# First norm with its mean in PSUM, later norms and a convolution reworked around PSUM

## The chip, the cores and the metric

The kernel runs on one core of a Trainium2 chip. The metric is device time in microseconds of one execution; the time before is 1544.75 us, the median of three runs (1543.83, 1544.75 and 1547.15). A core has five engines, each with an instruction queue of its own that runs in order: PE (TensorE, with its weight loads shown as PEld), DVE (VectorE), ACT (ScalarE), POOL (GpSimd) and SP, which issues most of the DMAs. Engines wait for each other through semaphores.

## The reference

One step of a decoder with two layers, for 512 prompt positions and 8 x 8 sample positions, 576 tokens in all, with a model width of 1024. Layer 0 mixes with RWKV-7 and retention heads, layer 1 with a gated convolution; each mixer is followed by a squared-ReLU MLP, and each of the four residual sums by a layer norm. Cut to what the change touches:

```python
def layer_norm(x, g, b):
    mu = jnp.mean(xf, -1, keepdims=True)
    var = jnp.mean(jnp.square(xf - mu), -1, keepdims=True)
    return ((xf - mu) * lax.rsqrt(var + LN_EPS)).astype(x.dtype) * g + b

def conv_mixer(x, buf0, w_in, conv_w, w_out):
    bg, cg, h = jnp.split(x @ w_in, 3, axis=-1)
    u = cg * h
    ext = jnp.concatenate([buf0.astype(u.dtype), u], axis=1)
    conv = sum(ext[:, j:j + T] * conv_w[j] for j in range(CONV_W))
    return (bg * conv) @ w_out, ext[:, ext.shape[1] - (CONV_W - 1):]

# trunk, for layers l = 0 and 1
x = layer_norm(ALPHA * x + y, ln1_g[l], ln1_b[l])            # norms 0 and 2
x = layer_norm(ALPHA * x + sqrelu_mlp(x, w_up[l], w_down[l]), ln2_g[l], ln2_b[l])   # norms 1 and 3
```

## The kernel before

**Layout.** Features lie on partitions: `T.x` is eight row tiles of 128 features x 576 tokens, and most work goes by halves of the tokens, g = 0 and 1, of 288 each (`GN`). An f32 product is made of three matmuls of a rounded high part and a low part (`mm3`): high x high, high x low, low x high. Each operand is therefore split, as a rule by a cast on ScalarE (L77) and a subtraction on VectorE (L78), and both parts are kept.

**Order of the work.** Layer 0's mixers run until about 430 us; their instructions are placed by hand-written generators. The scheduler of the framework then orders each engine's queue by priorities and its own estimate of times, so a change of a few instructions can reorder a queue beyond the lines that the diff names. The output projection (`Wout`) runs among the mixers in three parts, over the input blocks k = 0 to 2, 3 to 5, and 6, and adds into `T.x`; the last block, k = 7, is done at the start of the trunk with the weights `w7`, together with the first norm. Then come MLP 1, norm 1, the convolution's input projection (three columns of row tiles by an ordinary product, the other six in nine seven-product steps), its output projection with norm 2, MLP 2, and norm 3, whose outputs leave by DMA.

**The first norm.** Because a mean over features is linear in the weights, `means` takes the column means of the weights of k = 6 and 7, and these are subtracted from the weights (`less`), so what those blocks add has no mean. `center`, run after the second part, sums the eight row tiles with matmuls against a constant 1/1024 (L1395) and subtracts the result from `T.x` (L1396). In the trunk, `ln0_add` (L289) adds each product of k = 7, squares the sum on ScalarE (L291), adds pairs of squares on POOL (L294) and sums over features with an f32 matmul against 1/1024 (L283). `ln0_finish` makes the factor and scales.

**Norms 1 to 3.** `ln_add` takes the row tiles as they are finished (L257), and adds up both the tiles and their squares on POOL and VectorE (L273); one matmul against 1/1024 for each of the two sums turns these into mean and mean square in PSUM. `ln_finish` copies the mean out of PSUM (L322), makes the factor v, subtracts the mean (L341), multiplies by v on VectorE or POOL (L342) and applies gain and offset on ScalarE (L345), followed by the split.

**Seven products.** `gemm7` makes two row tiles for both token halves from seven products of half the depth (12 matmuls each) in place of eight. Every product has a PSUM bank of its own, out of six; two are copied to SBUF on ScalarE (L207, L213), and the sums are built in SBUF by five adds on VectorE and two on POOL (all L205). In the convolution an `evac` function is then called on the two finished tiles `ta` and `tb`: a gate (kept), the product u = gate x h with the convolution behind it on ScalarE and VectorE (L1721 to L1723), or the product with the third tile, which is split for the output projection.

Of the kernel before, what the change touches and what calls it, by code (L numbers as in the profile page):

```python
# [16 lines left out]
P = 128  # L17
# [7 lines left out]
class Trunk:  # L25
# [124 lines left out]
    def mm3(self, acc, hi, lo, xh, xl, first, last):  # L150
        nc = self.nc
        nc.tensor.matmul(acc, lhsT=hi, rhs=xh, start=first, stop=False)  # L152
        nc.tensor.matmul(acc, lhsT=hi, rhs=xl, start=False, stop=False)  # L153
        nc.tensor.matmul(acc, lhsT=lo, rhs=xh, start=False, stop=last)  # L154
# [68 lines left out]

    def ln_state(self, n, x):
        return {'n': n, 'x': x}
# [37 lines left out]
    def ln_sum(self, st, n, m, g, t, direct, onv):  # L263

        nc = self.nc
        if m in direct:
            self.ln_mm(st, n, g, t, m == KT - 1 and (g, n) not in st)
# [7 lines left out]
        if m == KT - 1 and (g, n) in st:  # L275
            self.ln_mm(st, n, g, st[g, n], True)
# [8 lines left out]
    def ln0_add(self, st, m, g, r, a):  # L285

        nc = self.nc
        st[g, m] = r
        nc.vector.tensor_tensor(out=r, in0=r, in1=a, op=ALU.add)  # L289
        t = self.p_tmp.tile([P, GN], F32, tag="t", name="lt", bufs=self.tb)  # L290
        nc.scalar.activation(t, r, AF.Square)  # L291
        if m >= 6: self.ln_mm(st, 'q', g, t, m == 7)
        elif m % 2:
            nc.gpsimd.tensor_tensor(out=t, in0=st[g, 'q'], in1=t, op=ALU.add)  # L294
            self.ln_mm(st, 'q', g, t, False)
        else: st[g, 'q'] = t
# [19 lines left out]

    def ln_finish(self, st, g, par, out, last=False):
        nc = self.nc
# [995 lines left out]
CFG = {(n, g): dict(ds=() if n else tuple(range(8)), dq=() if n else tuple(range(8)), sv=(7,), qv=(7,), pg=(1, 2, 3, 4, 5, 6, 7), mulv=(0, 3, 6), affv=()) for n in range(4) for g in range(2)}  # L1314
# [11 lines left out]
class Wout:  # L1326


    def __init__(self, T, w):
        self.T, self.nc, self.w = T, T.nc, w  # L1330
        self.w7, self.less = [], {}
# [12 lines left out]
    def weights(self, m, k0, n):  # L1344

        t = self.slot()
        b = self.less.get(k0)
        if b is None:
            t = t[:, 0:n]
            self.nc.sync.dma_start(t.rearrange('p m c -> p (m c)'), self.w[30 + m, :, P * k0:P * (k0 + n)])  # L1350
        else:
            n = 2
            self.nc.sync.dma_start(t, self.w[30 + m:32 + m, :, P * k0:P * (k0 + 1)].rearrange('m p c -> p m c'))
            self.nc.scalar.activation(t, t, AF.Identity, bias=b)
        hi, lo = (self.wq.tile([P, 2, P], F32R, tag=f'w{c}', name=c, bufs=3)[:, 0:n] for c in 'hl')
# [4 lines left out]
    def means(self):  # L1360
# [3 lines left out]

        def load(k, m):
            t = self.slot()
            nc.sync.dma_start(t, self.w[30 + m:32 + m, :, P * k:P * (k + 1)].rearrange('m p c -> p m c'))
            return t
        for k in (6, 7):
            s = self.wq.tile([P, 4], F32, name=f's{k}', bufs=1)  # L1370
            for m in range(0, 8, 2):
                t = load(k, m)
                nc.vector.tensor_reduce(out=s[:, m // 2:m // 2 + 1], in_=t, axis=AX.XY, op=ALU.add)
            b = self.wq.tile([P, 1], F32, name=f'b{k}', bufs=1)
            nc.vector.tensor_reduce(out=b, in_=s, axis=AX.X, op=ALU.add)
            nc.vector.tensor_scalar(out=b, in0=b, scalar1=-1.0 / 1024, scalar2=None, op0=ALU.mult)
            self.less[k] = b
        for m in range(0, 8, 2):
            t = load(7, m)
# [6 lines left out]
    def center(self, mx):  # L1386
# [3 lines left out]
        nc.gpsimd.memset(o, 1 / 1024)  # L1390
        for g in range(2):
            ps = mx.tile([P, 512], F32, tag='mx', name='mx')[:, 0:GN]
            xs = [t[:, GN * g:GN * (g + 1)] for t in T.x]
            for m, t in enumerate(xs):
                nc.tensor.matmul(ps, lhsT=o, rhs=t, start=m == 0, stop=m == KT - 1)  # L1395
# [405 lines left out]
```

## Time and profile before

| | |
|---|---|
| runs | 1543.83, 1544.75, 1547.15 us |
| profiled execution | 1545.83 us, of which the span takes 1544.1 |
| mean granted clock of TensorE | 0.972 |
| first norm, from the last block's stall to the MLP's first matmul | 472.8 to 512.09 us |
| norm 1, second half | 911 to 929 us |
| convolution's seven-product steps | about 970 to 1070 us |
| norm 3, last product to last DMA | 1526.5 to 1544.1 us |

A row of the profile gives the line of the kernel, the engine, the operation, the tiles it writes and reads, and their size; a bracket at its end gives the time that the engine stood idle before it and what it waited for. In a table of waits a row gives the total in microseconds, the number of waits and the longest. Matmuls are pipelined: one of 128x288 is shown with 0.29 us, but the next starts 0.13 us after it.

### The profile page before, as it was taken

What the parts mean: (1) busy time and instruction counts of PE and PEld (TensorE: products, weight loads), DVE (VectorE), ACT (ScalarE), POOL (GpSimd) and SP (SyncE); (2) the same over time, 40 slices, a digit from 0 to 9 for tenths busy, and PEclk for the clock granted to TensorE, in tenths of its full rate; (3) what the DMA queues carried; (4) which work ended last, traced back from release to release, by engine and by line L of the source; (5) the groups of instructions that cost most, each with busy time, mean ns of one, the idle gap of its engine ahead of it and who ended that gap; (6) DMA issues with size and microseconds to landing.
All of it is one profiled execution on the core that took longest, in us unless ns stands there. A gap on an engine that the chain in (4) does not pass through costs nothing.

```text
span 1544.1 us, 29826 instructions
## 1 busy us (share of the span) xinstructions
PE 1464.9 (95%) x11744; PEld 1414.5 (92%) x11744; DVE 1072.2 (69%) x2040; ACT 643.6 (42%) x1355; POOL 547.9 (35%) x619
## 2 busy tenths in 40 slices
PE   6999999999997899999999989999989999999995
PEld 6998898989786899999999989989989999999995
DVE  4655676766868884855748689899799475574845
ACT  4433334233343851523525454334366253351533
POOL 2032213346442531212113665554682131121355
PEclk9999999999998999999999999999999999999998
DMA  5332334445322131322313302223304223142211
GB/s 173 98 97 86 94 97 132 137 115 168 117 61 81 42 123 55 100 93 70 123 56 111 122 1 69 83 83 113 109 1 123 69 83 110 55 127 66 96 56 62
DMA packets 73244, 141.08 MB, mean 91 GB/s; under 512 B 21744, under 2 KB 33248, under 8 KB 73104
## 3 DMA queue, kind: packets, MB, share of 16 engines
q1 hardware_dynamic: 70272, 130.74, 27.4%
q0 software_dynamic: 1536, 5.57, 1.1%
q10 hardware_dynamic: 1296, 2.86, 0.5%
q8 instruction: 92, 1.51, 0.4%
q14 instruction: 48, 0.39, 0.1%
HBM read 125.44 MB, written 13.70 MB: 90 GB/s over the span
## 4 chain that ended last, share of the span: by engine, by line
PE 73%; DVE 11%; issue 5%; POOL 4%; DMA 4%; ACT 2%; SPq 1%; DVEq 0%; ACTq 0%; POOLq 0%
PE acc L152 20%; PE acc L153 20%; PE acc L154 20%; DVE wl L78 3%; PE mx L835 2%; DMA raw<-in_w 1%; POOL x L255 1%; DVE u L341 1%; PE mx L732 1%; POOL ts L1653 1%; PE mx L574 1%; PE wa L152 1%; ACT wh L77 1%; POOL ln L273 1%; PE mx L524 1%
## 5 line engine op out<-in xcount | busy, mean ns | idle before, releaser
L77 ACT CAST wh<-raw 128x512 fp32r<-128x512 f32 x440 | 252.7, 618 | 421.1 <-PE acc L153 271.0
L78 DVE TENSOR_TENSOR wl<-raw,wh 128x512 fp32r<-128x512 f32 x440 | 334.0, 791 | 42.0 <-ACT wh L77 35.0
L153 PE MATMUL acc<-hl,wh 128*128 128x288 f32 x1180 | 348.9, 297 | 0.0
L154 PE MATMUL acc<-hh,wl 128*128 128x288 f32 x1180 | 348.6, 296 | 0.0
L152 PE MATMUL acc<-hh,wh 128*128 128x288 f32 x1180 | 346.2, 297 | 1.9 <-DVE ta L205 1.8
L152 PEld LDWEIGHTS acc<-hh,wh 128*128 128x128 f32 x1180 | 221.0, 188 | 2.8 <-DVE ta L205 2.0
L153 PEld LDWEIGHTS acc<-hl,wh 128*128 128x128 f32 x1180 | 222.2, 188 | 0.5
L154 PEld LDWEIGHTS acc<-hh,wl 128*128 128x128 f32 x1180 | 222.2, 188 | 0.3
L152 PE MATMUL acc<-xh,wh 128*128 128x288 f32 x480 | 147.7, 309 | 14.1 <-ACT xh L1482 12.4
L153 PE MATMUL acc<-xl,wh 128*128 128x288 f32 x480 | 145.6, 304 | 0.0
L123 POOL TENSOR_TENSOR s<-raw 128x512 f32<-128x512 f32 x37 | 52.0, 1405 | 264.0 <-DMA raw<-in_w 197.6
L154 PE MATMUL acc<-xh,wl 128*128 128x288 f32 x480 | 145.5, 303 | 0.0
L153 PE MATMUL acc<-lt,wh 128*128 128x288 f32 x444 | 131.8, 297 | 3.6 <-DVE lt L78 3.6
L154 PE MATMUL acc<-ht,wl 128*128 128x288 f32 x444 | 131.6, 296 | 0.9 <-DVE wl L78 0.9
L152 PE MATMUL acc<-ht,wh 128*128 128x288 f32 x444 | 131.3, 296 | 0.1
L123 POOL TENSOR_TENSOR raw<-raw 128x512 f32<-128x512 f32 x37 | 54.9, 1484 | 158.9 <-DVE raw L123 106.4
L152 PEld LDWEIGHTS acc<-xh,wh 128*128 128x128 f32 x480 | 90.9, 190 | 17.7 <-ACT xh L1482 12.7
L152 PE MATMUL acc<-ho,wh 128*128 128x288 f32 x352 | 104.6, 297 | 0.1
L154 PE MATMUL acc<-ho,wl 128*128 128x288 f32 x352 | 104.6, 297 | 0.0
L153 PE MATMUL acc<-lo,wh 128*128 128x288 f32 x352 | 104.5, 297 | 0.0
L153 PEld LDWEIGHTS acc<-xl,wh 128*128 128x128 f32 x480 | 90.9, 189 | 2.5 <-DVE xl L1483 0.7
L154 PEld LDWEIGHTS acc<-xh,wl 128*128 128x128 f32 x480 | 91.0, 190 | 1.5 <-issue 0.2
(485 smaller groups left out, 3466.6 us busy)
## 6 DMA issues: line engine op xcount, KB each, us to landing
raw<-in_w SPq DMA_DIRECT2D x160, 512.0 KB, 3.6
raw<-in_w SPq DMA_DIRECT2D x60, 256.0 KB, 2.9
la<-in_w SPq DMA_DIRECT2D x32, 128.0 KB, 2.2
A<-stg SPq DMA_DIRECT2D x9, 288.0 KB, 2.5
x<-in_x POOLq DMA_DIRECT2D x8, 288.0 KB, 5.8
out_y<-x SPq DMA_DIRECT2D x16, 144.0 KB, 1.8
kr<-A SPq DMA_DIRECT2D x6, 288.0 KB, 2.8
lr<-in_x ACTq DMA_DIRECT2D x4, 288.0 KB
```

Of the source, the lines that this page charges most:

```text
L77: a = self.nc.scalar.copy(hi[:, s], src[:, s])
L78: b = self.nc.vector.tensor_tensor(out=lo[:, s], in0=src[:, s], in1=hi[:, s].bitcast(F32), op=ALU.subtract)
L123: tt = lambda e, o, x, y, op: e.tensor_tensor(out=o, in0=x, in1=y, op=op)
L152: nc.tensor.matmul(acc, lhsT=hi, rhs=xh, start=first, stop=False)
L153: nc.tensor.matmul(acc, lhsT=hi, rhs=xl, start=False, stop=False)
L154: nc.tensor.matmul(acc, lhsT=lo, rhs=xh, start=False, stop=last)
L255: e.tensor_tensor(out=t, in0=t, in1=c, op=ALU.subtract)
L273: (nc.vector if m in onv else nc.gpsimd).tensor_tensor(out=o, in0=st[g, n], in1=t, op=ALU.add)
L341: nc.vector.tensor_tensor(out=u, in0=r, in1=mn, op=ALU.subtract)
L524: self.nc.tensor.matmul(out, lhsT=src, rhs=self.C['ident'][q, q], start=True, stop=True)
L574: self.nc.tensor.matmul(ps, lhsT=lhsT, rhs=rhs[:, o:o + n], start=True, stop=True)
L835: nc.tensor.matmul(ps[:, i], lhsT=bd(self.mb if n < 3 else self.Y0, j + i), rhs=v[:, j + i], start=True, stop=True)
```

## The change

Six edits, all around where a sum is held.

1. `means` computes the column means of the weights of k = 7 only. The weights of k = 6 are no longer centred.
2. `center` runs after the third part of the output projection, so the mean is that of all of k = 0 to 6. It is not subtracted from `T.x`: it is split into a high and a low part (`W.mean`), and in the trunk each product of k = 7 begins with two matmuls of a negated identity (`W.neg`) by these parts, so the mean is subtracted in PSUM.
3. The squares of the first norm are all summed on TensorE, row tile by row tile; POOL's adds are gone.
4. In norms 1 to 3, for the second half of the tokens, the row tiles 6 and 7 and their squares go straight to TensorE; the sum of tiles 0 to 5 is added as before.
5. For that half `ln_finish` is replaced by `ln_end`: mean and factor stay in PSUM, the row tile is changed in place, and no product is left to POOL. The first half keeps the old way.
6. The convolution's nine steps use `chained7`: products that are added to each other are accumulated onto the same bank, three banks for seven products, with copies of what stands in between on ScalarE, three adds on VectorE and none on POOL. The last sum is read from PSUM by `evac`. The copies of the new convolution state go from POOL to ScalarE.

`mm3` is written more shortly and issues the same matmuls. The core of the diff:

```diff
@@ Trunk
+    def chained7(self, u, x7, evac):
...
+        a = product(0, bank())
+        nc.scalar.copy(s1, a)
+        c = product(3, bank())
+        nc.scalar.copy(s5, c)
+        product(2, a, False)
+        nc.scalar.copy(u2, a)
+        product(5, c, False)
+        add(ta[:, r], c, u2)
+        product(4, a, False)
+        add(tb[:, r], a, s5)
+        b = product(1, bank())
+        add(ta[:, l], b, s1)
+        evac(0, ta, None)
+        product(6, a, False)
+        evac(1, tb, a)
@@ ln_add
-        if m == KT - 1 and (g, n) in st:
-            self.ln_mm(st, n, g, st[g, n], True)
+        if m not in direct and (m == KT - 1 or m + 1 in direct):
+            self.ln_mm(st, n, g, st[g, n], m == KT - 1)
@@ ln0_add
-        if m >= 6: self.ln_mm(st, 'q', g, t, m == 7)
-        elif m % 2:
-            nc.gpsimd.tensor_tensor(out=t, in0=st[g, 'q'], in1=t, op=ALU.add)
-            self.ln_mm(st, 'q', g, t, False)
-        else: st[g, 'q'] = t
+        self.ln_mm(st, 'q', g, t, m == KT - 1)
+    def ln_end(self, st, par, out, last):
...
+        mean, v = st[1, 's', 'ps'], st[1, 'q', 'ps']
+        nc.scalar.activation(d, mean, AF.Square)
+        V.scalar_tensor_tensor(out=v, in0=v, scalar=LN_EPS, in1=d, op0=ALU.add, op1=ALU.subtract)
+        with self.tc.issue_after(self.pre.ins):
+            nc.scalar.activation(w0, v, AF.Ln)
+        nc.scalar.activation(w, w0, AF.Exp, scale=-0.5)
+        sub = lambda r: V.tensor_tensor(out=r, in0=r, in1=mean, op=ALU.subtract)
+        for m in range(3): sub(st[1, m])
+        V.scalar_tensor_tensor(out=w0, in0=w, scalar=-0.5, in1=w, op0=ALU.mult, op1=ALU.mult)
+        V.tensor_tensor(out=v, in0=v, in1=w0, op=ALU.mult)
+        V.scalar_tensor_tensor(out=v, in0=v, scalar=1.5, in1=w, op0=ALU.add, op1=ALU.mult)
+        for m in range(KT):
+            r, b = st[1, m], bet[:, m:m + 1]
+            if m > 2: sub(r)
+            V.scalar_tensor_tensor(out=r, in0=r, scalar=gam[:, m:m + 1], in1=v, op0=ALU.mult, op1=ALU.mult)
+            if last:
+                if m in (3, 6): V.tensor_scalar(out=r, in0=r, scalar1=b, scalar2=None, op0=ALU.add)
+                else: nc.scalar.activation(r, r, AF.Identity, bias=b)
+                out(m, 1, r)
+                continue
+            hi, lo = out(m, 1)
+            x = nc.scalar.activation(hi, r, AF.Identity, bias=b)
+            y = V.scalar_tensor_tensor(out=lo, in0=r, scalar=b, in1=hi.bitcast(F32), op0=ALU.add, op1=ALU.subtract)
+            nc.scalar.activation(r, r, AF.Identity, bias=b)
@@ CFG, for n in range(4) for g in range(2)
-ds=() if n else tuple(range(8)), dq=() if n else tuple(range(8))
+ds=(6, 7) if g else (), dq=(6, 7) if g else ()
@@ Wout.means
-        for k in (6, 7):
...
+        for m in range(0, 8, 2):
+            t = self.slot()
+            nc.sync.dma_start(t, self.w[30 + m:32 + m, :, P * 7:P * 8].rearrange('m p c -> p m c'))
+            nc.vector.tensor_reduce(out=s[:, m // 2:m // 2 + 1], in_=t, axis=AX.XY, op=ALU.add)
+            ts.append(t)
@@ Wout.center
+        self.neg = self.wq.tile([P, P], F32R, name='neg', bufs=1)
+        nc.scalar.activation(self.neg, self.ident, AF.Copy, scale=-1.0)
...
-            for t in xs: nc.vector.tensor_tensor(out=t, in0=t, in1=ps, op=ALU.subtract)
+            nc.scalar.copy(self.mean[0][:, s], ps)
+            nc.vector.tensor_tensor(out=self.mean[1][:, s], in0=ps, in1=self.mean[0][:, s].bitcast(F32), op=ALU.subtract)
@@ wout
-                    if n == 1: W.center(mxb)
+                    if n == 2: W.center(mxb)
@@ trunk
-            T.mm3(a, hi, lo, *hx(7, g), True, True)
+            for n in range(2): nc.tensor.matmul(a, lhsT=W.neg, rhs=W.mean[n][:, gs[g]], start=n == 0, stop=False)
+            T.mm3(a, hi, lo, *hx(7, g), False, True)
@@ evac_in7
-        def f(j, t):
+        def f(j, t, a):
+            z = 0 if a is None else GN
...
+                if z: mul(V, u[:, 2:2 + z], a, cgt[j][:, 0:z])
+                mul(nc.gpsimd, u[:, 2 + z:514], t[:, z:512], cgt[j][:, z:512])
...
-            T.gemm7(102 + 3 * k + 2 * w, x7, evac_in7(k, w))
+            T.chained7(102 + 3 * k + 2 * w, x7, evac_in7(k, w))
```

The order of the instructions moves at three places that matter. First VectorE around the first norm. Before, where the block for k = 6 begins, the subtractions of the mean (`mx`) from the row tiles end, and the adds of that block's sums (`wa`) follow:

```order
L1396 TENSOR_TENSOR x5_4553<-x5_4553,mx_5906 128x288
L1396 TENSOR_TENSOR x6_4554<-x6_4554,mx_5906 128x288
L1396 TENSOR_TENSOR x7_4555<-x7_4555,mx_5906 128x288
L1425 TENSOR_TENSOR x0_4548<-x0_4548,wa_5927 128x288
L586 SCALAR_TENSOR_TENSOR rsa_6043<-hv_6021,rsa_6043 128x10
L1425 TENSOR_TENSOR x0_4548<-x0_4548,wa_5928 128x288
```

After, at the end of that block, VectorE makes the low parts of the MLP's first weights (`wl` from `raw`) between the last adds, and the low parts of the mean (`mlo`) behind them:

```order
L1484 TENSOR_TENSOR x6_4554<-x6_4554,wa_5931 128x288
L78 TENSOR_TENSOR wl_6097<-raw_6086,wh_6096 128x512 x2
L1484 TENSOR_TENSOR x6_4554<-x6_4554,wa_5932 128x288
L78 TENSOR_TENSOR wl_6105<-raw_6088,wh_6104 128x512
L1484 TENSOR_TENSOR x7_4555<-x7_4555,wa_5958 128x288
L78 TENSOR_TENSOR wl_6105<-raw_6088,wh_6104 128x512
L1484 TENSOR_TENSOR x7_4555<-x7_4555,wa_5959 128x288
L78 TENSOR_TENSOR wl_6113<-raw_6090,wh_6112 128x512 x2
L1454 TENSOR_TENSOR mlo_5984<-mx_5985,mhi_5983 128x288
L1454 TENSOR_TENSOR mlo_5984<-mx_5996,mhi_5983 128x288
```

The sixteen subtractions are gone, and the mean's low half now stands behind casts that need the loads of `raw`. Second, TensorE at the same place. Before, the products of k = 7 (`acc` from `hh`, the high part of k = 7's input) already begin between the last sums of k = 6:

```order
L154 MATMUL wa_6009<-hi6_5923,l_5984 128x288
L152 MATMUL acc_6188<-hh7_6140,kh0_5449 128x288
L152 MATMUL acc_6195<-hh7_6140,kh0_5449 128x288
L152 MATMUL acc_6205<-hh7_6140,kh2_5455 128x288
L152 MATMUL wa_6010<-hi6_5923,h_5983 128x288
L153 MATMUL wa_6010<-lo6_5924,h_5983 128x288
```

After, the products of the mean (`mx`) end the block, and the negated identity with the mean's two parts opens every bank:

```order
L152 MATMUL wa_5959<-hi6_5831,l_5935 128x288
L1452 MATMUL mx_5996<-x6_4554,wo_5979 128x288
L1452 MATMUL mx_5985<-x7_4555,wo_5979 128x288
L1452 MATMUL mx_5996<-x7_4555,wo_5979 128x288
L1766 MATMUL acc_6120<-mhi_5983,neg_5981 128x288
L1766 MATMUL acc_6120<-mlo_5984,neg_5981 128x288
L152 MATMUL acc_6120<-hh7_6072,kh0_5416 128x288
L152 MATMUL acc_6120<-hl7_6073,kh0_5416 128x288
```

No product of k = 7 is started ahead of the mean any more. Third, ScalarE at the start of the convolution's seven-product steps. Before, two copies of a bank (`s1`, `s5`) a step stand among the casts of weights (`wh`, `vh`):

```order
L207 COPY s1_11328<-acc_11331 128x288
L77 CAST wh_11320<-raw_11142 128x512 x2
L77 CAST vh_11316<-s1_11305 128x512
L213 COPY s5_11330<-acc_11373 128x288
L77 CAST wh_11435<-raw_11295 128x512 x2
```

After, there are three (`s1`, `s5`, `u2`), and two of them read the same bank:

```order
L244 COPY s1_11282<-acc_11285 128x288
L77 CAST vh_11270<-s1_11259 128x512
L246 COPY s5_11284<-acc_11299 128x288
L77 CAST wh_11274<-raw_11096 128x512 x2
L248 COPY u2_11283<-acc_11285 128x288
```

What moved is the number of copies, and that a bank is written again behind its copy.

More of the change, by code (lines that the diff above doesn't have):

```diff
@@ L148, in mm, with mm3 @@
         self.mm3(acc, *self.split[u][k], x[k][0][:, s], x[k][1][:, s], first, last)
[L150 to L154, printed above, removed]
+    def mm3(self, acc, hi, lo, xh, xl, first, last, onto=False):
+        mm = lambda w, x, a, b: self.nc.tensor.matmul(acc, lhsT=w, rhs=x, start=a, stop=b, skip_group_check=onto)
+        mm(hi, xh, first, False)
+        mm(hi, xl, False, False)
+        mm(lo, xh, False, last)
     def gemm(self, u0, n, x, evac, head=0, tail=0, after=None, early=False, far=0):
@@ L222, in steps7, with product, add @@
         yield
+    def chained7(self, u, x7, evac):
+        nc, pt = self.nc, self.p_tmp
+        self.ensure(u + 1)
+        self.ensure(u + 1 + self.ahead)
+        ta, tb = [self.wide(n) for n in ('ta', 'tb')]
+        s1, u2, s5 = [pt.tile([P, GN], F32, tag='t', name=n, bufs=self.tb) for n in ('s1', 'u2', 's5')]
+        l, r = slice(0, GN), slice(GN, NT)
+        bank = lambda: self.p_acc.tile([P, GN], F32, tag="acc", name="acc")
+        def product(i, acc, first=True):
+            for k in range(KT // 2):
+                self.mm3(acc, *self.split[u][i][k], *x7[i][k], first and k == 0, k == KT // 2 - 1, onto=not first)
+            return acc
+        def add(o, x, y):
+            nc.vector.tensor_tensor(out=o, in0=x, in1=y, op=ALU.add)
+        a = product(0, bank())
[13 more added lines that the diff above has]
+        evac(1, tb, a)
+        del self.split[u]
     def ln_state(self, n, x):
@@ L266, in ln_sum @@
         if m in direct:
-            self.ln_mm(st, n, g, t, m == KT - 1 and (g, n) not in st)
+            self.ln_mm(st, n, g, t, m == KT - 1)
         elif (g, n) not in st:
@@ L1311, in drive @@
     tc.cur_priority = base + max(p for _, p in SCHEDULE) + 10000
[L1314 removed]
+CFG = {(n, g): dict(ds=(6, 7) if g else (), dq=(6, 7) if g else (), sv=(7,), qv=(7,), pg=(1, 2, 3, 4, 5, 6, 7), mulv=(0, 3, 6), affv=()) for n in range(4) for g in range(2)}
 FAR1, FAR2 = 3, 4
@@ L1330, in __init__ @@
         self.T, self.nc, self.w = T, T.nc, w
-        self.w7, self.less = [], {}
+        self.w7 = []
         self.slots = self.staged = 0
@@ L1413, in part @@
                 n = min(2, len(ks) - j)
-                if ks[j] not in self.less: hi, lo = self.weights(m, ks[j], n)
-                elif m % 2 == 0: two = self.weights(m, ks[j], n)
-                if ks[j] in self.less: hi, lo = (w[:, m % 2:m % 2 + 1] for w in two)
+                if n == 2: hi, lo = self.weights(m, ks[j], True)
+                else:
+                    if m % 2 == 0: one = self.weights(m, ks[j], False)
+                    hi, lo = (w[:, m % 2:m % 2 + 1] for w in one)
                 for g, a in enumerate(accs):
```

66 lines of the change are left out of this document (30 added, 36 removed).

## The prediction

> **What bounds the kernel now.** I read the page's head first, for the span, the engines and the clock.
>
> ```profile
> span 1544.1 us, 29826 instructions
> PE 1464.9 (95%) x11744; PEld 1414.5 (92%) x11744; DVE 1072.2 (69%) x2040; ACT 643.6 (42%) x1355; POOL 547.9 (35%) x619
> ...
> PE 73%; DVE 11%; issue 5%; POOL 4%; DMA 4%; ACT 2%; SPq 1%; DVEq 0%; ACTq 0%; POOLq 0%
> ```
>
> TensorE is busy 95% of 1544.1 us and holds 73% of the chain that ended last. So an edit is worth only what it takes from TensorE's waits, its half-clock time or its own instructions. Next I read the table by stretches, whose columns are length, busy time of PE, PEld, DVE, ACT, POOL, granted clock, DMA share and rate, for the places that the change touches.
>
> ```profile
> 472.00:480.00 8.00, 1.19 (x7) 0.91 (x6) 7.93 (x23) 0.00 (x0) 1.38 (x3) 0.71 0.00 1
> 480.00:490.00 10.00, 9.61 (x39) 8.13 (x39) 7.38 (x20) 2.15 (x4) 1.69 (x5) 0.55 0.12 26
> 490.00:512.00 22.00, 15.80 (x77) 12.35 (x76) 19.47 (x43) 14.15 (x35) 6.92 (x7) 0.87 0.48 159
> 512.00:850.00 338.00, 335.18 (x2504) 334.35 (x2503) 225.35 (x376) 151.35 (x291) 82.24 (x69) 0.99 0.28 86
> 912.00:930.00 18.00, 13.40 (x84) 12.71 (x83) 16.56 (x25) 11.75 (x26) 12.39 (x13) 0.81 0.05 10
> 970.00:1070.00 100.00, 93.78 (x671) 92.62 (x669) 91.60 (x127) 40.33 (x77) 55.99 (x63) 0.95 0.28 85
> 1118.00:1150.00 32.00, 29.41 (x205) 28.73 (x204) 30.55 (x43) 21.05 (x51) 23.95 (x25) 0.95 0.01 2
> 1200.00:1500.00 300.00, 300.00 (x2259) 299.79 (x2258) 182.46 (x310) 117.81 (x217) 69.76 (x64) 1.00 0.27 85
> 1526.00:1544.10 18.10, 2.04 (x8) 0.79 (x6) 9.59 (x18) 7.03 (x15) 7.67 (x9) 0.61 0.25 87
> ```
>
> The two MLP stretches are full at full clock: they pass a shift on unchanged. What can be won lies in five places: the first norm (472 to 512), norms 1 and 2 (912, 1118), the convolution's seven-product steps (970 to 1070, where VectorE is at 92% too) and the tail. The waits of TensorE there, as total, times, longest:
>
> ```profile
> PE wa L152 <- DVE x L1425: 6.8, 1, 6.8
> PE pq L283 <- POOL lt L294: 2.7, 1, 2.7
> ...
> PE acc L152 <- ACT hh L77: 3.5, 1, 3.5
> PE acc L153 <- DVE hl L78: 3.3, 2, 2.2
> ...
> PE acc L152 <- DVE ta L205: 7.4, 3, 3.7
> ```
>
> The first two are the first norm, the middle two norm 1, the last the convolution. All sums below go against the profiled execution, 1545.83 us, which is 1.08 us above the median of the runs shown, 1544.75.
>
> **Part 1: the means of the weights.** `means` drops four of eight column reductions and eight of twelve loads; four ScalarE operations on the weights of k=6 go too, beside which nothing waited.
>
> ```profile
> L1373 DVE TENSOR_REDUCE s<-la x8: 404/412/421, 408.3 to 422.5; 128x1 f32<-128x256 f32 x8
> ```
>
> The eight stand over 14 us between 408.3 and 422.5, and VectorE's only gaps there are waits for these loads. Four reductions are 4 x 0.41 = 1.6 us, the two small ones behind them 0.3. VectorE feeds TensorE in this stretch, but TensorE has its own work too: between 0 and 3 us, I take **-2**.
>
> **Part 2: mean and squares of the first norm.** These rows carry it.
>
> ```profile
> 466.01 1.62 PE L1395 MATMUL mx<-x,wo 128*128 128x288 f32 x6
> 467.47 0.27 PE L976 MATMUL mx<-cst,rot 128*64 128x128 f32 x1
> ...
> 470.05 0.29 PE L152 MATMUL wa<-hi,h 128*128 128x288 f32 x1
> 470.18 0.29 PE L153 MATMUL wa<-lo,h 128*128 128x288 f32 x1
> ...
> 471.20 0.51 PE L152 MATMUL wa<-hi,h 128*128 128x288 f32 x1
> ...
> 473.32 5.91 DVE L1396 TENSOR_TENSOR x<-x,mx 128x288 f32<-128x288 f32 x16
> ...
> 479.65 0.61 PE L152 MATMUL wa<-hi,h 128*128 128x288 f32 x1 [6.81 <-DVE x L1425]
> ...
> 487.08 0.75 DVE L1198 SCALAR_TENSOR_TENSOR y<-y,hd 128x576 f32<-128x576 f32 x1
> ...
> 498.35 1.14 ACT L77 CAST wh<-raw 128x512 fp32r<-128x512 f32 x2 [1.49 <-DMA raw<-in_w]
> ...
> 512.09 1.29 PE L152 MATMUL acc<-he,wh 128*128 128x288 f32 x4
> ```
>
> A product against the ones is two instructions of f32: six instructions start in 1.46 us (466.01 to 467.47), so 0.243 each and 0.486 for one product. A 128x288 matmul of the split kind starts 0.13 us after the one before it.
>
> Before, 16 mean products stand ahead of the block for k=6 and 16 subtractions behind them (5.91 us of VectorE), for which TensorE waits 6.81 us. After, the block starts 15 products earlier, at about 471.2 - 15 x 0.486 = 463.9. It now takes 48 x 0.133 + 16 x 0.486 = 14.2 us, and about 1.1 us of a head's matmuls among them: it ends near 479.2. The subtractions are gone, but the mean is needed before the next step, as two casts. In VectorE's new order the small half of the mean stands behind eight casts of the MLP's first weights (four loads). These loads start once y7 is done (487.83 before, 10.5 us ahead of the fourth load's cast at 498.35). After, the last operation on y7 stands behind the adds of the third row tile: 5.9 us of TensorE, then two adds and y7's own 0.75 on VectorE and the hand-overs, some 8.2 us in all, so 472.1. The fourth load's cast then starts at 482.6; that pair of casts (1.14), VectorE's half of them and the first mean half make 2.3 us more: TensorE goes on near **484.9**, having waited 5.7 us. So the old wait of 6.8 is nearly replaced by a new one, for another reason.
>
> From there come 16 x 5 matmuls with the negated identity (32 more than before, 4.3 us) and 16 products of squares (6 more, 2.9 us): 10.6 + 7.8 = 18.4 us, ending at 503.3 at full clock. The six POOL adds, and the 2.7 us waited for them, go. The MLP began at 512.09, when the last squares of the second half were done; it should begin when these are. Clock: the stretch from 480 to 490, behind the old wait, ran at 0.55, which cost 10 x 0.45 = 4.5 us. Bounds 0 and 4.5 for the new one; I take 3, nearer the row, because the new stretch is denser. 503.3 + 3 = 506.3, so **-5.8**; ends: -13 (the mean is not held by the loads) and 0 (POOL's and VectorE's casts of the weights hold the sums as well).
>
> The Trainium skill ("TensorE: Matmul & The Clock Gate", Part 1: The HAM clock gate) says that the clock halves after an idle window of about 3.4 us and is back after about 3.4 us of busy time. By that the loss would be an estimated 1.7 us and the MLP would begin at 505.0; the row above, 0.55 over 10 us, shows more, and goes ahead of it.
>
> **Part 3: norms 1 and 2, second half of the tokens.**
>
> ```profile
> L342 DVE TENSOR_TENSOR u<-u,ln x18: 445/1056/1068, 899.3 to 1538.4; 128x288 f32<-128x288 f32 x18
> L342 POOL TENSOR_TENSOR u<-u,ln x30: 878/1016/1038, 899.2 to 1538.5; 128x288 f32<-128x288 f32 x30
> ...
> L205 DVE TENSOR_TENSOR ta<-acc,s x74: 440/446/459, 551.9 to 1468.3; 128x288 f32<-128x288 f32 x74
> ...
> 920.48 1.09 PE L152 MATMUL acc<-hh,ht 128*128 128x288 f32 x3 [3.46 <-ACT hh L77]
> 922.70 0.61 PE L153 MATMUL acc<-hl,ht 128*128 128x288 f32 x1 [1.14 <-DVE hl L78]
> ```
>
> A VectorE product of two SBUF tensors takes 1.056 us beside POOL's multiplications and 0.445 alone (least, median, most of L342); one that reads PSUM and SBUF is never above 0.459 (L205). The new end of the norm keeps mean and factor in PSUM and lets POOL out, so its eight subtractions and eight products cost 0.37 and 0.43 apiece in a row. Added are four products against ones, 4 x 0.486 = 1.9 us, which fall ahead of the old wait and so come out of it. Chain after: the squares are summed at about 913.2 as before, then square of the mean, Ln, Exp and three small operations (4 us), eight products (3.4 us), and the first low half near 922.0, against 922.70. The later waits for hl and lo (2.2 and 0.6) lose their 1.06 us operations, and the clock (0.81 from 912 to 930) a little of its fall. That is **-2** for norm 1 and **-2** for norm 2, each between +1 (the added sums are not hidden) and -4.
>
> The Trainium skill ("SBUF — State Buffer", Who interferes with whom) says that a VectorE instruction with two SBUF inputs contends with a GpSimd one that reads SBUF, and one with at most one SBUF input does not. The rows of L342 and L205 agree. Without it the products could cost 1.06 beside POOL's remaining work, 8 x 0.6 = 4.8 us more by an estimate from L342, and each norm would be 2.8 us slower instead.
>
> **Part 4: the convolution.** Nine steps of seven products. Per step two POOL adds go (0.81 us median) and two VectorE adds (0.45 each); three multiplications move from POOL to VectorE, one for each of three pairs. VectorE's load over the 100 us falls by about 18 x 0.45 - 5 x 0.45 = 6 us, POOL's by 18 x 0.81 = 15. Small state copies go from POOL to ScalarE, which is at 40 of 100 us. TensorE's waits for L205 (7.4 us) should shrink, and with them the low clock. New: a product that goes onto a used bank must wait until ScalarE has copied it (three copies a step, 0.39 us). The scheduler puts another product between, 12 x 0.133 = 1.6 us, so a prompt copy is hidden. Ends -7 and, if it isn't prompt, the rival's price; I take **-3**.
>
> **Part 5: the tail.**
>
> ```profile
> 1526.47 0.45 DVE L257 TENSOR_TENSOR x<-x,acc 128x288 f32<-128x288 f32 x1 [1.84 <-PE acc L154]
> ...
> 1538.87 2.18 ACT L345 ACTIVATE x<-u,par 128x288 f32<-128x288 f32 x4 [1.10 <-DVE u L342]
> ```
>
> From the last product (1526.47) to the last output (1541.05) are 14.6 us, then 3 us of output DMA, unchanged. After: two products of the mean stand ahead of the last matmul (+1.0), two adds of VectorE and two of POOL go, the squares are complete near 1529.5, the factor near 1532.5 and then eight products, five subtractions and two additions on VectorE, 8 x 0.43 + 5 x 0.37 + 2 x 0.3 = 5.9 us, and ScalarE's last 0.5: 1538.9, so **-2.2** (0 to -4).
>
> **Sum.** -2 - 5.8 - 2 - 2 - 3 - 2.2 = -17.0, that is 1528.8 for an execution like the profiled one and **1527.7** for the median.
>
> **Rivals.**
> *ScalarE's copies come late (slower).* In the convolution ScalarE runs its queue in order, and a copy stands behind a cast of weights that waits for its loads and sums:
>
> ```profile
> ACT wh L77 <- POOL raw L123: 20.6, 6, 8.4
> ...
> ACT wh L77 <- DVE raw L123: 2.8, 1, 2.8
> ...
> ACT wh L77 <- DMA raw<-in_w: 1.3, 1, 1.3
> ```
>
> These 24.7 us cost TensorE nothing so far. If all of them reach it through the copies, the conv is +24.7 instead of -3: 1545.8 - 14.0 + 24.7 = 1556.5, or 1555.4 for the median. It decides from a copy 1.6 us late, and the whole is slower once 14 of the 24.7 us arrive. Against it: POOL, which those casts wait for, loses 15 us of work. Chance 0.10.
> *The waits only change their name.* First norm and norms 1 and 2 give nothing, since the mean waits for the weights' loads and the added products (2.9 + 4.3 + 3.9 us) fill what was idle: -7.2 remain, 1537.5 for the median. Chance 0.22.
> *Nothing is left.* Besides that, the conv stays bound by VectorE (91.6 of 100 us) and the means' 2 us are waited for elsewhere: the tail's -2.2 alone, 1542.5 for the median. Chance 0.08.
> *All waits go.* The mean isn't held and the clock holds: -13 for the first norm, -7 in the conv, 1516.5. Chance 0.08.
>
> **How the numbers follow.** Forecast 0.52, around 1522 to 1534. A measurement of this kernel can tell about 0.2%, 3.1 us. Faster by more than that: forecast, renamed waits and all waits gone, 0.82; within it 0.08; slower 0.10. The range goes from 1516 to 1546: below and above it lie the late copies and the last of the deep case, under 0.15.
>
> **What would show it.** The wait before the first matmul of the negated identity should name VectorE's mean half and lie near 479 to 485; the MLP's first matmul stand near 506 less the gain of part 1; hl's wait of norm 1 fall below 1 us; no wait of TensorE on ScalarE's copies; the last product to the last output take 12.5 us. A wait of TensorE on a copy in the convolution, or a first norm whose wait is over 8 us, would make the prediction wrong.

## The result, and the profile after

The changed kernel takes 1534.75 us (median of five runs, 1530.86 to 1539.90) against 1546.09 us for the kernel before, run beside it (1543.83 to 1547.35). The ratio is 0.9922, with a 95% interval from 0.9903 to 0.9941: 11 to 12 us faster, where 17 were forecast. The page's head after the change:

```profile
span 1533.0 us, 29786 instructions
PE 1465.6 (96%) x11812; PEld 1416.3 (92%) x11812; DVE 1043.6 (68%) x2019; ACT 647.4 (42%) x1365; POOL 495.0 (32%) x554
```

TensorE is as busy as before (1464.9 us then) in a span 11.1 us shorter, although it runs 68 instructions more. Two things went: its idle time fell from 79.2 to 67.4 us, and its mean granted clock rose from 0.972 to 0.985, which by an estimate from these two is some 43 us lost to the clock before (0.028 of the span) and 23 now. Part of that is spent again on the added instructions. VectorE lost 29 us of work and POOL 53, but these count only where TensorE waited for them. The table by stretches, with the columns as before:

```profile
430.00:465.00 35.00, 34.42 (x342) 30.29 (x338) 20.35 (x53) 11.71 (x29) 12.67 (x17) 0.94 0.18 57
465.00:472.00 7.00, 4.54 (x27) 3.66 (x27) 6.54 (x19) 2.01 (x5) 3.20 (x4) 1.00 0.00 0
472.00:480.00 8.00, 8.00 (x39) 6.73 (x38) 4.71 (x14) 2.15 (x4) 1.68 (x5) 0.79 0.07 17
480.00:490.00 10.00, 8.48 (x42) 5.81 (x40) 8.95 (x18) 5.16 (x10) 0.00 (x0) 1.00 0.80 265
490.00:512.00 22.00, 21.24 (x130) 19.22 (x131) 14.48 (x35) 12.51 (x31) 1.28 (x1) 1.00 0.13 46
530.00:550.00 20.00, 16.19 (x100) 15.73 (x100) 20.00 (x23) 12.91 (x28) 14.35 (x12) 0.84 0.17 54
912.00:930.00 18.00, 14.98 (x96) 14.21 (x95) 16.95 (x36) 11.93 (x26) 4.39 (x4) 0.91 0.24 70
970.00:1070.00 100.00, 96.06 (x715) 94.66 (x714) 80.20 (x132) 49.08 (x107) 35.22 (x38) 1.00 0.32 101
```

The first norm (472 to 512) is now nearly full, the convolution (970 to 1070) full at full clock with VectorE at 80 in place of 92 of 100 us. New holes show at 465 to 472 and at 530 to 550. TensorE's longest waits, over the whole run (the first row is of the kernel's start, where it was 12.4 before, in code that is the same):

```profile
PE acc L152 <- ACT xh L1541: 13.3, 2, 7.1
PE acc L152 <- ACT s L244: 6.1, 1, 6.1
PE acc L152 <- ACT wh L77: 5.2, 2, 4.5
...
PE acc L152 <- DVE lt L78: 3.8, 2, 2.5
PE acc L152 <- ACT u L248: 3.4, 4, 2.1
PE wa L152 <- DVE x L1484: 2.2, 3, 1.6
PE rpo L1227 <- DVE rS L1220: 1.9, 1, 1.9
...
PE acc L1766 <- DVE mlo L1454: 1.5, 1, 1.5
PE acc L152 <- DVE hl L376: 1.5, 2, 1.2
```

The 6.8 us on the mean, the 2.7 on POOL's squares and the 7.4 on `ta` are gone. In their place stand waits on ScalarE's copies in the convolution (`s`, `u`: 9.5 us), which the prediction priced in a rival only.

To put the difference in its places I cut both executions at the same landmarks on TensorE. Each number is the start of one instruction less the start of the one before it in the list:

| stretch, up to | before | after | difference | forecast |
|---|---|---|---|---|
| unchanged first part, 0 to the first product with `rkm` | 366.60 | 367.28 | +0.7 | 0 |
| third group of products with `rkm` (means of the weights) | 65.89 | 67.53 | +1.6 | -2 |
| last product with `rot` (block k = 6 about to begin) | 34.98 | 29.93 | -5.0 | with the next |
| the MLP's first product (end of the first norm) | 44.62 | 44.24 | -0.4 | -5.8 for both |
| norm 1's first sum (end of MLP 1) | 380.93 | 383.08 | +2.2 | 0 |
| norm 1's first low half | 29.68 | 30.26 | +0.6 | with the next |
| norm 2's first `cps` product, called the convolution's last sum below | 162.96 | 156.15 | -6.8 | -5 for both |
| norm 2's first sum, and its first low half | 57.61 | 57.23 | -0.4 | with the next |
| norm 3's first sum (norm 2's rest and MLP 2) | 369.80 | 368.25 | -1.6 | -2 for both |
| end | 31.03 | 29.05 | -2.0 | -2.2 |

The sum is -11.1, as the spans say, 5.9 us short of the 17.0 forecast. The first 900 us fall 6.9 short: 3.6 at the means, 2.2 in MLP 1, 0.4 in the first norm and 0.7 in code that is the same in both; behind them 1.0 more is won than forecast, nearly all in the convolution. One landmark needs care: `cps` belongs to the output projection's first row tile, and how many matmuls the scheduler puts ahead of it differs between kernels. In the unchanged first part the profiled executions of all kernels below take between 363.9 and 369.8 us, so a difference of a few microseconds there, in one pair of executions, shows nothing.

### The profile page after: what moved, and what is told of

Its sections match the earlier page's. It is cut to its first block, busy times and chain, and to the rows that moved or that the text cites. A ratio compares the mean times of both kernels' runs of the same rounds, so it can differ in the third digit from the quotient of the medians.

```text
span 1533.0 us, 29786 instructions
## 1 busy us (share of the span) xinstructions
PE 1465.6 (96%) x11812; PEld 1416.3 (92%) x11812; DVE 1043.6 (68%) x2019; ACT 647.4 (42%) x1365; POOL 495.0 (32%) x554
## 5 line engine op out<-in xcount | busy, mean ns | idle before, releaser
L78 DVE TENSOR_TENSOR wl<-raw,wh 128x512 fp32r<-128x512 f32 x440 | 325.9, 773 | 50.9 <-ACT wh L77 44.0
L152 PEld LDWEIGHTS acc<-ht,wh 128*128 128x128 f32 x444 | 85.0, 192 | 16.4 <-ACT s L244 6.4
```

The costliest lines, as they stand in the source:

```text
L78: b = self.nc.vector.tensor_tensor(out=lo[:, s], in0=src[:, s], in1=hi[:, s].bitcast(F32), op=ALU.subtract)
L152: mm = lambda w, x, a, b: self.nc.tensor.matmul(acc, lhsT=w, rhs=x, start=a, stop=b, skip_group_check=onto)
```

## The experiments

Twelve kernels, all of the changed program with something put back or moved; all compute the whole reference. The edits are numbered as in the description of the change, the parts as in the prediction; the diffs are cut to their core. The ratio is to the kernel before, run beside them, with its 95% interval.

| kernel | ratio | interval |
|---|---|---|
| the change | 0.9922 | 0.9903 to 0.9941 |
| x1: convolution with `gemm7` again | 0.9942 | 0.9927 to 0.9956 |
| x2: first norm as before (edits 1 to 3 undone) | 0.9924 | 0.9910 to 0.9937 |
| x3: norms 1 to 3 as before (edits 4 and 5 undone) | 0.9905 | 0.9890 to 0.9919 |
| x4: mean taken after part 2 again, but held in PSUM | 0.9910 | 0.9894 to 0.9927 |
| x5: first of the nine steps by `gemm7` | 0.9903 | 0.9887 to 0.9919 |
| x6: squares added on POOL again | 0.9899 | 0.9886 to 0.9913 |
| x7: x4 and x5 | 0.9879 | 0.9862 to 0.9895 |
| x8: x4, x5 and x6 | 0.9907 | 0.9892 to 0.9921 |
| x9: only norm 1 as before | 0.9894 | 0.9876 to 0.9913 |
| x10: x4 and x9 | 0.9891 | 0.9875 to 0.9908 |
| x11: copies `u2` on VectorE | 0.9913 | 0.9898 to 0.9929 |
| x12: x7 with x11 | 0.9875 | 0.9859 to 0.9891 |

**x1, x2 and x3: which of the three groups gives the gain.**

```diff
 x1
-            T.chained7(102 + 3 * k + 2 * w, x7, evac_in7(k, w))
+            T.gemm7(102 + 3 * k + 2 * w, x7, evac_in7(k, w))
...
 x2
-        self.ln_mm(st, 'q', g, t, m == KT - 1)
+        if m >= 6: self.ln_mm(st, 'q', g, t, m == 7)
...
-                    if n == 2: W.center(mxb)
+                    if n == 1: W.center(mxb)
...
 x3
-        if g: return self.ln_end(st, par, out, last)
...
```

> The changed kernel with the convolution's steps put back to seven separate products (part 6 undone, all else kept). Forecast's term (-3 for the convolution): span about 1536 against 1533.0, and the stretch from the first low half of norm 1 to the convolution's last sums (156.2 us in the changed kernel, 163.0 before) about 159. If the whole of that stretch's gain (6.8 us) is the chained products: 163 and a span near 1540. Rival, that the chained products cost as much as they give, since TensorE waited 9.9 us there for ScalarE's copies: 154 to 156 and a span of 1531 to 1533.

> The changed kernel with the first norm's mean and squares put back as before (parts 1 to 3 undone). Forecast's terms (-2 and -5.8): span about 1541. By the stretches of the two traces (3.1 us won up to the first matmul of MLP 1, 2.15 lost again inside MLP 1): span about 1534, with the first matmul of MLP 1 near 512 and the first sum of norm 1 near 893.

> The changed kernel with the end of norms 1 to 3 put back (parts 4 and 5 undone). Forecast's terms (-2, -2 and -2.2): span about 1539, the tail from the last first-half sum to the end 31 us in place of 29.05, the low half's waits in norms 1 and 2 back at 1 to 2.3 us. Rival, that the added sums on TensorE eat what the shorter chain wins in norms 1 and 2: only the tail's 2 us, span about 1535.

Without the chained products 0.20 points of the 0.78 go; the intervals still overlap, but the trace below agrees. Without the new first norm, or the new ends of the later norms, the kernel is not slower beyond the intervals. Added up, the three account for 0.05 of the 0.78 points, with intervals about as wide as what they are to tell, so the ratios don't say where the gain comes from. The traces, one execution each, do: undone, each part's stretch goes back to about what it was before. In x2 the first norm's two stretches take 79.6 us and MLP 1 380.9, in x3 the tail 30.7 (31.0 before), in x1 the convolution's 161.3. x3's span, 1534.4 us, is near what its rival had (1535): beside the tail the old ends cost nothing in the whole, since the convolution is shorter there. In the table by stretches, the convolution of x1:

```profile
970.00:1070.00 100.00, 89.37 (x640) 88.45 (x639) 90.32 (x130) 41.62 (x81) 57.86 (x64) 0.95 0.27 88
```

and that of x3, with the chain and the old ends of the norms:

```profile
970.00:1070.00 100.00, 98.38 (x734) 97.17 (x734) 81.15 (x133) 50.86 (x110) 35.16 (x39) 1.00 0.30 102
```

x1 has VectorE at 90 of 100 us and the clock at 0.95 again, as before, and TensorE's longest wait there is on VectorE's adds once more:

```profile
PE acc L152 <- DVE ta L206: 10.6, 3, 4.9
```

In x3 the stretch from norm 1's first low half to the convolution's last sum takes 152.63 us, against 162.96 before, 156.15 with the change and 161.28 in x1. So the chain gives 10.3 us beside the old norms, but only 5.1 (161.28 - 156.15) beside the new ones, where TensorE stands still at the first step. The row of the changed kernel's timeline (start, length, instruction, idle time ahead):

```profile
962.69 0.61 PE L152 MATMUL acc<-ht,wh 128*128 128x288 f32 x1 [6.13 <-ACT s L244]
```

and ScalarE's queue at that time:

```profile
960.12 0.43 ACT L77 CAST hh<-yc 128x288 fp32r<-128x288 f32 x1 [2.51 <-DVE yc L1794]
960.87 1.14 ACT L77 CAST wh<-raw 128x512 fp32r<-128x512 f32 x2 [0.32 <-POOL raw L123]
961.92 0.43 ACT L77 CAST hh<-yc 128x288 fp32r<-128x288 f32 x1
962.25 0.39 ACT L244 COPY s<-acc 128x288 f32<-128x288 f32 x1
```

The copy that frees the bank stands last in a queue that waits for VectorE's `yc`. TensorE, which must write on the same bank, has 23 matmuls between in the change's order, 23 x 0.133 = 3.1 us, and then stood still for 6.1 us more. In x3 ScalarE has the same four instructions in the same order, but TensorE's order holds 33 matmuls between, and there is no wait on `s`; all waits on ScalarE's copies in the convolution come to 0.3 us there, against 9.5. The ten more matmuls are only 1.3 us of that: TensorE also comes to this product later against ScalarE's queue, so the copy begins 4.1 us behind the start of the product's last matmul, where it was 9.0.

**x5: the first step without the chain.**

```diff
-            T.chained7(102 + 3 * k + 2 * w, x7, evac_in7(k, w))
+            f = evac_in7(k, w)
+            if k == 2 and w == 0: T.gemm7(102 + 3 * k + 2 * w, x7, lambda j, t: f(j, t, None))
+            else: T.chained7(102 + 3 * k + 2 * w, x7, f)
```

> The changed kernel with the first of the nine convolution steps as seven separate products, the other eight chained. Theory: the 6.1 us that TensorE waits at 962.69 for ScalarE's copy s come from the chaining alone, since the copy stands behind a cast that waits for VectorE, and a separate bank needn't wait for it. Then that wait falls below 1.5 us, the stretch from the first low half of norm 1 to the convolution's last sums goes from 156.2 to 151 to 153, the median to about 1530. Rival, that VectorE holds this place and the wait only moves on to the adds: the stretch stays at 155 to 157.

The wait on `s` is gone, and the stretch falls from 156.15 to 153.12 us. The row at the same place:

```profile
963.19 0.40 PE L152 MATMUL acc<-ht,wh 128*128 128x288 f32 x1 [0.59 <-DVE yc L1794]
```

Of 6.1 us waited for, 3.0 are won: the waits on `u` grow from 3.4 to 6.2. So a separate bank takes this wait away, as the theory had it, and half of it comes back at the other steps.

**x9 and x10: is it norm 1's new end?** x9 puts only norm 1's end back; x10 does so with the mean of x4.

```diff
-        if g: return self.ln_end(st, par, out, last)
+        if g and st['n'] != 1: return self.ln_end(st, par, out, last)
...
```

> The changed kernel with the end of norm 1 alone put back; norms 2 and 3 keep the new end. Theory: under the chained steps norm 1's new end costs about 5 us between its first low half and norm 2's first sum, because it leaves ScalarE later at the convolution's first copy; norms 2 and 3 keep their gain. Then the stretch from the first sum of norm 1 to norm 2's first sum is 208 to 210 us (213.6 in the changed kernel, 208.5 with all norms put back), the tail stays at 29 us, median about 1530. Rival, that the 5 us came from the other norms or from the scheduler's order by chance: 212 to 214.

> The same with the early mean. If the two are independent: from the last rot product to the first matmul of MLP 1 37 us, the stretch of norm 1 and the convolution 208 to 210, the tail 29; median 1524 to 1528, below every other kernel here. If the early mean is only luck of the order, it stays at 1530.

From norm 1's first sum to norm 2's first sum the change takes 213.6 us, x3 208.5, x9 208.1 and x10 213.1. So x9 wins the 5 us and x10, which has the same end of norm 1, does not: the scheduler gave x10 the ScalarE order of the changed kernel in the convolution's steps, and x9 that of x3. In the second step, for one, four weight casts and another copy stand ahead of `u2` in x10, and in x9 it comes right behind `s5`. TensorE's waits on the copies, x10 first, then x9:

```profile
PE acc L152 <- ACT u L248: 3.6, 4, 2.2
...
PE acc L152 <- ACT s L244: 1.8, 1, 1.8
```

```profile
PE acc L152 <- ACT s L244: 1.1, 1, 1.1
...
PE acc L152 <- ACT u L248: 0.3, 1, 0.3
```

The 5 us belong to an order of the queues that small edits elsewhere switch, not to the arithmetic of norm 1's end.

**x11 and x12: is the place of `u2` in ScalarE's queue what costs?**

```diff
-        nc.scalar.copy(u2, a)
+        nc.vector.tensor_copy(u2, a)
```

> Only the nine copies u2 go from ScalarE to VectorE; the first step's s1 copy stays behind the casts of yc. Theory (the 3.4 us of TensorE's waits on u2 come from ScalarE's order, where two casts of weights and a copy stand ahead of u2): these waits fall below 1 us, the wait on s1 stays at 4 to 6 us, and the stretch from the first low half of norm 1 to the convolution's last sum falls from 156.2 to about 153.5; ratio to before about 0.991. Rival (the copy is late wherever it is made, and VectorE at 80% is the busier engine): TensorE waits for VectorE's u2 and ta by 3 us or more, and the stretch stays at 156 or grows.

> The mean taken before block 6, the first of the nine steps without chaining, and the u2 copies of the other eight on VectorE. Theory: the 4.4 us of waits on ScalarE's u2 shrink, the stretch from the first low half of norm 1 to the convolution's last sum falls from 152.0 to about 150, ratio to before about 0.987. Rival (VectorE takes over as what is late): 152 to 155, ratio 0.988 or above.

My theory fell, and its rival fits better. TensorE's waits in x11's convolution:

```profile
PE acc L152 <- ACT s L244: 5.1, 1, 5.1
PE acc L152 <- DVE tb L242: 1.7, 3, 0.8
PE acc L152 <- DVE u L248: 1.6, 2, 1.1
```

The waits on `u` and `tb` together are 3.3 us, against 3.9 with the change, and 5.9 in x12, against 4.7 in x7: the copy is hardly earlier on the busier engine. The stretch grows from 156.15 to 158.84 us, and from 152.02 in x7 to 155.28 in x12, but part of that is the landmark: in x11 and x12 TensorE runs 22 more matmuls of later work ahead of `cps`. Up to norm 2's first low half, with 1472 matmuls in each of the four, x11 takes 214.50 us against 213.38 with the change, and x12 210.94 against 209.24 in x7, so 1.1 and 1.7 us more. x12's ratio is x7's within the interval.

**x4: the mean early, but in PSUM.** The weights of k = 6 are centred again, and the mean is taken after part 2.

```diff
-                    if n == 2: W.center(mxb)
+                    if n == 1: W.center(mxb)
...
```

> The changed kernel with the mean taken after the second part of the output projection, as before (block 6's weights centred again, four more column means), but still put into PSUM through the negated identity, with no subtraction from the row tiles. Theory: in the changed kernel block 6 starts at 467.8 and stalls until 471.7 because its input is not ready, and the 16 mean products (7.8 us), which stood in that time before, now come behind it. Then here block 6 still starts near 468 to 472, its matmuls take 8 us, the negated identity begins near 480 and the first matmul of MLP 1 at 499 to 503 (508.98 in the changed kernel, 512.09 before); of these 6 to 9 us MLP 1 gives back some 2, so span 1526 to 1529. Rival, that VectorE and the weights' loads hold the first norm whatever the order: first matmul of MLP 1 at 507 to 510 and a span of 1532 to 1535.

The first norm from the `rot` landmark to the MLP falls from 44.24 to 37.28 us: no wait for the mean is left. The stretch ahead of it grows from 29.93 to 37.01, since its 16 mean products stand there again. Together the two take 74.3 us, no less than with the change (74.2), and neither the expected 499 to 503 us for MLP 1's first matmul nor the expected span came (512.31 and 1536.4). But the clock in the mixers (0.66, 0.58 and 0.74 in three stretches of 10 us) was low in this execution, and its median is 1531.85 where the profiled execution took 1538.17. In the other kernels with x4's edit and the new squares, x7, x10 and x12, the two stretches together take 71.6, 71.7 and 72.4 us, against 74.2 for the change and 79.6 before: 1.8 to 2.5 us better. What ends the first norm in x4 are the squares:

```profile
502.97 4.12 PE L319 MATMUL pq<-lt,o 128*128 128x288 f32 x16 [0.57 <-DVE x L1493]
508.54 4.15 PE L319 MATMUL pq<-lt,o 128*128 128x288 f32 x16 [1.46 <-ACT lt L327]
```

**x6, x8: the squares on POOL again**, without and with the early mean.

```diff
-        self.ln_mm(st, 'q', g, t, m == KT - 1)
+        if m >= 6: self.ln_mm(st, 'q', g, t, m == 7)
+        elif m % 2:
+            nc.gpsimd.tensor_tensor(out=t, in0=st[g, 'q'], in1=t, op=ALU.add)
+            self.ln_mm(st, 'q', g, t, False)
+        else: st[g, 'q'] = t
```

> The changed kernel with the squares of the first norm added in pairs on POOL again (part 3 undone). The forecast has the six more products of TensorE at 2.9 us against 2.7 us of waiting for POOL. If TensorE is the bound of the first norm since the change, the first matmul of MLP 1 comes 2 to 3 us sooner after the last rot product (44.2 us in the changed kernel). If POOL's adds hold it again, 44 to 46.

> The early mean, the first separate step and the squares in pairs on POOL. With the early mean the 16 products of squares stand as two blocks of 4.1 us at the end of the first norm with nothing beside them; with the pairs they are 5 products each. Theory: from the last rot product to the first matmul of MLP 1 34 to 35 us instead of 37.3, median 1524 to 1527. Rival, that POOL's adds come as late as before (2.7 us): 37 to 38.

In x6 the first norm takes 43.75 us, 0.5 less than with the change: as long as the mean comes late, POOL's sums are in time, and summing the squares on TensorE gives nothing. In x8, with the early mean, it takes 39.60 where x7 takes 36.68, longer than either expectation, and the old wait is back:

```profile
508.03 4.67 PE L319 MATMUL pq<-lt,o 128*128 128x288 f32 x10 [2.72 <-POOL lt L330]
```

So the edit is worth 2.9 us, but only once the wait ahead of it is gone.

**x7: the best of the parts.** x7 has the edits of x4 and x5.

> The early mean and the first separate step together. If both work by themselves: from the last rot product to the first matmul of MLP 1 37 us, and 151 to 153 from the first low half of norm 1 to the convolution's last sums; median 1527 to 1529.

1527.07 us (ratio 0.9879): faster than both kernels, by the gain in the first norm and the 4.1 us in the convolution. x12 (0.9875) is not told apart from it.

## Why the prediction was right, and where it was not

The sign, the range and most of the places were right; the forecast, 1527.7, was 7 us too low, and the rival of renamed waits, 1537.5, was 2.8 too high. That the total came out at two thirds of the forecast owes something to luck, since parts that gave less and one that gave more offset each other, and the range from 1516 to 1546 held all rivals but one. In the first norm and in norm 1 the rival is close to what the runs show: x2 and x3, which undo these parts (x3 norms 2 and 3 as well), can't be told from the change in time, and the added products fill what was idle. What it missed is the convolution, where the chain gave 5.1 us (the change against x1) for the 3 that both had.

Of the signs that I had named, the tail did better than said (11.2 us for 12.5), and the wait on the mean's low half has the right name but not the right time. The MLP's first matmul stood at 508.98, not near 506 or below, `hl`'s wait in norm 1 at 1.2 us, not below 1, and TensorE waited 9.5 us on ScalarE's copies in the convolution. By the prediction's own words that last sign makes its account of the convolution wrong, though the term came out larger. By the prediction's parts:

**Part 1 (-2): nothing.** TensorE's waits between 366 and 437 us add up to 5.3 us before and 5.7 after. One that was not there takes the place of two that were (1.3 on `rss`, now 0.9, and 1.3 on `hd`, now gone):

```profile
426.87 0.49 PE L1227 MATMUL rpo<-rS,e 128*128 128x128 f32 x2 [1.91 <-DVE rS L1220]
```

The stretch takes 65.3 to 68.3 us in the kernels with this part and 66.0 to 68.4 in those without (x2, x4, x7, x8, x10, x12): there is no gain to be seen in it. The failed step is "VectorE feeds TensorE in this stretch": what VectorE no longer did was not what TensorE waited for last.

**Part 2 (-5.8): the size right (-5.4), two steps wrong, which cancelled by luck.** In the seven kernels with the new mean taken late the two stretches of the table take 73.7 to 77.5 us, against 79.6 in both with the old first norm, so the 5.4 is one execution's out of 2.1 to 5.9. I let block 6 begin at 463.9 us, by taking 15 products off its old start. Its own input wasn't ready:

```profile
468.36 0.40 PE L152 MATMUL wa<-hi,h 128*128 128x288 f32 x1 [0.17 <-DVE x L1484]
469.31 0.40 PE L152 MATMUL wa<-lo,h 128*128 128x288 f32 x1 [0.55 <-POOL lo L1466]
...
471.69 0.40 PE L152 MATMUL wa<-hi,h 128*128 128x288 f32 x1 [1.57 <-DVE x L1484]
```

POOL's low half of the input (`lo`) comes some 4.5 us behind the `rot` product before and after: the mean products that stood there had been filling a wait. Now TensorE idled for 2.5 us of seven, and 472 to 480 ran at a clock of 0.79. On the other hand the wait on the mean's low half is where I had it in the order, but 1.5 us long, not 5.7, because the block itself ended late:

```profile
490.60 0.40 PE L1766 MATMUL acc<-mhi,neg 128*128 128x288 f32 x1 [1.49 <-DVE mlo L1454]
```

From there to the MLP's first product at 508.98 are 18.4 us, just the 18.4 of the sum (10.6 of products with the mean, 7.8 of squares), at a granted clock of 1.00: the 3 us kept for a half clock weren't needed there, and the 0.79 ahead cost 1.7 (0.21 x 8). The wait that I had named for 479 to 485 came at 490.

**MLP 1 (0): +2.2, in no step of mine.** "They pass a shift on unchanged" is not so for the first steps of an MLP. VectorE is busy all the 20.0 us from 530 to 550 (19.58 before), with what the norm left it, while POOL still makes `sums`:

```profile
540.39 0.40 PE L152 MATMUL acc<-lt,wh 128*128 128x288 f32 x1 [1.34 <-DVE lt L78]
...
544.32 0.61 PE L152 MATMUL acc<-lt,wh 128*128 128x288 f32 x1 [2.47 <-DVE lt L78]
```

Before there was one such wait, of 2.82 us; the clock there fell from 0.93 to 0.84. x2, with the old first norm, has the old 380.9 us in this stretch, and the eleven other kernels have 381.5 to 383.1. So of the first norm's 5.4 us some 2 are given back 30 us later in this execution, 0.6 to 2.2 over all, and the 3 left are about what the intervals can't tell (x2).

**Part 3 (-2 each): norm 2 -1.9, norm 1 about half at most.** In norm 1 the wait that I wanted below 1 us split into three:

```profile
919.05 0.67 PE L152 MATMUL acc<-hh,ht 128*128 128x288 f32 x3 [1.08 <-ACT hh L375]
920.41 0.40 PE L152 MATMUL acc<-he,wh 128*128 128x288 f32 x1 [0.69 <-ACT wh L77]
...
922.32 0.42 PE L152 MATMUL acc<-hl,ht 128*128 128x288 f32 x1 [1.24 <-DVE hl L376]
```

Their 3.0 us are less than the 3.46 and 1.14 of before, but the added sums of f32 take it back: 30.26 us to the first low half, against 29.68. The loss of those sums had been one end of my range (+1). Behind the first low half x1, which has this part without the chain, shows -1.7, so norm 1 is left with -1.1 in that execution. In norm 2 what remains is a wait for a weight cast, 4.5 us (the longest of `wh` in the table of waits).

The rule that I drew on, that of the Trainium skill ("SBUF — State Buffer", Who interferes with whom), shows once more. VectorE's low halves read two SBUF operands:

```profile
1136.36 0.52 DVE L376 SCALAR_TENSOR_TENSOR hl<-x,par,hh 128x288 fp32r<-128x288 f32 x1
...
1141.40 1.06 DVE L376 SCALAR_TENSOR_TENSOR hl<-x,par,hh 128x288 fp32r<-128x288 f32 x1
```

The second lies beside POOL's sums, and takes twice as long:

```profile
1141.12 1.02 POOL L1712 TENSOR_TENSOR ts<-x,x 128x288 f32<-128x288 f32 x1
```

So the case agrees with the rule that two such instructions contend, and the low halves weren't freed of it. Whether the factor in PSUM freed the products isn't shown by this execution: they take 0.51 us each, but no POOL instruction runs beside any of the 24. The other half of the rule shows in the kernel before, where L205's adds, with one input in PSUM, take 0.44 to 0.46 us with POOL's work beside them and without.

**Part 4 (-3): the gain was -10.3 and a new wait took a part of it.** Products and adds went as said, and VectorE fell from 91.6 to 80.2; the -10.3 is x3 against before, -5.1 the change against x1. The half clock went with the waits: from norm 1's first low half to the convolution's last sum the granted clock is 0.93 before, 0.95 in x1, 0.97 with the change and in x3. The step that failed is "the scheduler puts another product between, 12 x 0.133 = 1.6 us, so a prompt copy is hidden": there were 23 matmuls between, 3.1 us, but the copy wasn't prompt. This is the mechanism of the slower rival, at one place of nine. Its price, though, was not the 24.7 us of ScalarE's waits but 6.1 at the first step and 3.4 at the others, and 3 to 5 us of time (x5, x9). That x3 and x9 escape it is shown; why the scheduler's order differs, and how much of the 5 us each wait carries, stays open, since x11 more than halved one of them without gaining by it.

**Part 5 (-2.2): -2.0.** From the last add of a product to the last output:

```profile
1518.31 0.46 DVE L293 TENSOR_TENSOR x<-x,acc 128x288 f32<-128x288 f32 x1 [2.81 <-PE acc L152]
...
1525.40 3.49 DVE L368 SCALAR_TENSOR_TENSOR x<-x,par,pq 128x288 f32<-128x288 f32 x8
...
1528.93 0.54 ACT L371 ACTIVATE x<-x,par 128x288 f32<-128x288 f32 x1 [0.32 <-DVE x L368]
```

That is 11.2 us where I had 12.5 and before 14.6; the eight products take 0.44 each, as said, but all eight subtractions are done ahead of the factor, so the five that the sum had put behind it (1.85 us) cost nothing. The two added sums cost 1.0 ahead of it, as said, and the output's DMA 0.5 more.

## What to carry to other kernels

A wait that ends last covers others beside it: ask of each product that moves what will be ready when it is gone, its own inputs first, and price a moved block by its latest input, not by its old start less what stood ahead. Accumulating on a bank that a copy must first read saves adds, but ties TensorE to the queue of the engine that copies; count the matmuls that the scheduler really puts between, and look at what stands ahead of the copy. Parts of a change are not independent: undo them one by one and in pairs, since an edit can be worth nothing until another wait is gone (the squares, 2.9 us), and a part can cost what another gains.

## What was not expected of the hardware

Unchanged code differs between profiled executions by more than the edits in question: 363.9 to 369.8 us for the first part, in which all these kernels have the same order on TensorE but for at most a dozen of its 3291 matmuls. Behind it x4 and x7 have the same order, but for one small matmul, until the convolution, yet x4's granted clock is 0.58 in a stretch of the mixers of 10 us:

```profile
430.00:440.00 10.00, 8.72 (x113) 6.90 (x111) 6.02 (x12) 5.63 (x13) 5.83 (x12) 0.58 0.20 61
```

and x7's 0.71:

```profile
430.00:440.00 10.00, 9.47 (x97) 7.22 (x98) 6.40 (x13) 5.18 (x10) 6.31 (x8) 0.71 0.21 67
```

And a half clock did not follow every short stall: in the changed kernel, after 2.5 us idle between 465 and 472 it is seen (0.79 in the next 8 us), after the 1.5 us ahead of 490.60 it isn't (1.00).
